# Fourteen projection tiles of a fused decoder block in seven pairs, each by seven block products, with the attention's data through DRAM

## The chip, the cores and the metric

The kernel runs on one core of a Trainium2 chip. A core has a matrix engine (TensorE, PE in the profile; PEld is its weight load), VectorE (DVE), ScalarE (ACT), GpSimd (POOL) and SyncE (SP), which here only issues transfers. Matrix results land in PSUM, a small memory of eight banks; operands lie in SBUF. The metric is the device time in microseconds (us), the median of several runs.

## The reference, cut to what matters

One decoder block over 1024 tokens of width 1024:

```python
h = rms_norm(x, norm_w) * (1 + scale) + shift
proj = h @ w_in
qa, ka, va, za, beta_in, a_in, qb, kb, vb, zb, ga, gb = split(proj)
# mixer A: 8 heads of 128, convolution and SiLU on q, k, v, gated delta rule in chunks
y_A = (headwise_rms_norm(gated_delta_rule(q, k, v, g, beta)) * silu(za)) @ P_A
# mixer B: 12 heads of 64 in three groups with dilations 1, 4 and 16
#   (group 1: token t sees t-128..t; group 2: every 4th; group 3: every 16th)
y_B = (softmax_weighted(dilated_window_attention(qb, kb, vb)) * silu(zb)) @ P_B
merged = sigmoid(ga) * y_A + sigmoid(gb) * y_B
x = rms_norm(x + gate * (merged @ w_out), final_norm_w)
```

All of it is in float32, and the result is compared at that precision.

## The kernel before

**Tiles.** The modulated input h is kept transposed: eight tiles `hT[kk]` of 128 features x 1024 tokens. To keep float32 precision on the faster matmul format, every operand is split into a rounded part `hi` and a remainder `lo` (`activation` Copy on ACT, then a subtraction on DVE), and a product is three matmuls: hi x hi, hi x lo, lo x hi (`three`, line 593). A projection tile is 128 output features x 1024 tokens: 8 feature blocks x 3 terms x 2 halves of 512 tokens, 48 matmuls of 128x512 into the two banks of one `pj` buffer. Its weights arrive in a `wr` buffer (`w_load`, line 572), are split into two `wh` buffers (`w_split`, line 580), and its result goes to a consumer from `finish` (line 727).

**Order of the projections.** `prog` lists them: two gate tiles, then the tiles of the delta rule with gates between them (`ORDER`), then the last 18: query and key tiles of the three attention groups (q, k, q, k for each), then six z tiles. `projections` (line 772) works the list off. `out_store` (line 744) takes a buffer for the result before each tile; for the first query tile of a group it waits until `big` has four to spare.

**Buffers.** SBUF holds 34 `big` buffers of 128 x 1024 floats (16 of them are hT), 6 `mid` of half that, 2 `wr`, 6 `wh`. PSUM holds two `pj` of two banks and four `sb` of one.

**Who decides the order.** The file writes out every engine's instruction order itself. `Sched` (line 110) keeps a clock for each engine from a cost for each operation, and a list of streams (Python generators) with priorities; at each step it lets the ready stream of the smallest number go on. Projections have priority 99: they fill what the recurrences (3), the merges (3.5), the attention (6 to 7) and the splits for the output products (8) leave. On the chip each engine runs its instructions strictly in the order written, waiting where an operand is late. All transfers but one are issued by SP, in one queue.

**Attention.** `attn_group` (line 1319) loads the group's values from DRAM into two buffers, waits for its two query and two key tiles and for the group before, and lets two workers run eight units (`attn_unit`, line 1239): scores of two blocks of 128 queries for two heads, masked minimum on DVE, exponent on ACT, transposes on PE, product with the values, copy into `OG`. When all are done, `combine` (line 1364) weighs the groups against each other; `apply_gate` multiplies by z, `yb_split` splits.

**The tail.** `tail_products` (line 1580): the A branch's output product (`pa`, 8 tiles, reading `YA` from `ya_split`), the B branch's (`pb`, 8 tiles of 36 matmuls, reading `YB`), and the final product with `w_out`.

Of the kernel before, what the change touches and what calls it, by code (L numbers as in the profile page):

```python
# [30 lines left out]
)  # L31
NW = 8
# [17 lines left out]
class Slots:  # L50
# [28 lines left out]
    def put(self, n=1, t=None):  # L79
        for _ in range(n):  # L80
            self.free_at.append(self.s.cur_last() if t is None else t)

# [177 lines left out]
def hybrid_block_kernel(ctx: ExitStack, tc: tile.TileContext, x, c, norm_w, ada_w, ada_b, w_tiles, w_vb0, w_vb1,  # L260
# [50 lines left out]
    Xb = [const([P, 8, 64], f"Xb{i}") for i in range(2)]  # L311
# [7 lines left out]
    gate_d = [dp.tile([P, T], F32, name=f"gd{j}") for j in range(16)]  # L319
    row_d = dp.tile([1, T], F32, name="rowd")  # L320
# [81 lines left out]
    def consts_start():  # L402
        dve.memset(pw[:, 0], -0.5)
        dve.memset(pw[:, 1], 0.5)
        for i in range(2):
            pool.memset(TT[i], 0.0)
            pool.memset(Xb[i], 0.0)
        dve.memset(one_row, 1.0)
        yield ev_row

        pb = yield from pj.get()
        for hf in range(2):
            pe.matmul(pb[:, hf * 512:hf * 512 + 512], one_row, scb[1][0:1, hf * 512:hf * 512 + 512], start=True, stop=True)
        yield
        act.activation(pb, pb, AF.Silu)
        scb[2] = pb
        S.set(ev_mod)
        yield
        scb[0] = yield from big.get()
        act.activation(scb[0], pb, AF.Copy)  # L420
        big.put()
# [149 lines left out]

    def w_load():
        yield ev_loaded
        for u in units[FIRST:]:
            u.raw = yield from wr.get(shape=[P, u.n])
            sp.dma_start(u.raw, u.src)
            S.set(u.raw_ev)
            yield S.now()

    def w_split():  # L580
        for u in units[FIRST:]:
            yield u.raw_ev
# [9 lines left out]

    def three(pt, whi, wlo, khi, klo, first, last):
        for w, m, a, z in ((whi, khi, first, False), (whi, klo, False, False), (wlo, khi, False, last)):
            for hf in range(2):
                sl = slice(hf * 512, hf * 512 + 512)
                pe.matmul(pt[:, sl], w, m[:, sl], start=a, stop=z)
            yield S.now()


# [5 lines left out]
    QB, KB, VB, ZB = {}, {}, {}, {}  # L606
    ev_qb = [Event() for _ in range(6)]
    ev_kb = [Event() for _ in range(6)]
    ev_vb = [Event() for _ in range(3)]
    ev_zb = [Event() for _ in range(6)]  # L610
# [40 lines left out]
    def qk_out(pt, store, i, scale, ev):  # L651
        g = i // 2
        dst = store[i]
        if g:
            r = 4 if g == 1 else 8
            dst = dst.rearrange("p (r u) -> p r u", r=r)
        act.activation(dst, perm(pt, g), AF.Copy, scale=scale)
        pj.put()
        S.set(ev)
        return  # L660
        yield
# [10 lines left out]
    GT = {}  # L672
# [45 lines left out]
    for g_ in range(3):  # L718
        for i_ in (0, 1):
            feat("qB", 2 * g_ + i_)  # L720
            feat("kB", 2 * g_ + i_)
    for i_ in range(6):
        feat("zB", i_)
    for _ in range(len(gates)):
        gate_tile()

    def finish(kind, idx, pt):
# [8 lines left out]
        if kind == "zB":  # L736
            return silu_out(pt, ZB, idx, ev_zb[idx])
        if kind == "qB":
            return qk_out(pt, QB, idx, -0.125, ev_qb[idx])
        if kind == "kB":  # L740
            return qk_out(pt, KB, idx, 1.0, ev_kb[idx])
        return gate_out(pt, idx if kind == "gA" else 8 + idx)

    def out_store(kind, idx):
        st = dict(kA=KT, qA=QT, vA=VT, zA=ZT, qB=QB, kB=KB, zB=ZB, gA=GT, gB=GT)[kind]
        i = idx + 8 if kind == "gB" else idx
        add = dict(kA=4 - idx % 2, qA=1, qB=(4, 0, 4, 0, 4, 0)[idx % 6]).get(kind, 0)
# [24 lines left out]
    def projections():  # L772
# [39 lines left out]
        for n, (kind, idx, u) in enumerate(prog):  # L812
            if n < FIRST:
                continue
            lastp = n == len(prog) - 1
# [26 lines left out]
            if lastp:  # L842
                S.set(ev_tail)
            pt = yield from pj.get()
            yield u.ev
            for kk in range(8):
# [3 lines left out]
                if lastp:  # L850
                    big.put(2)
            wh.put(2)
            S.add(finish(kind, idx, pt), 10, f"{kind}{idx}")

        yield from tail_products()
# [57 lines left out]
    ev_ttfree = [Event() for _ in range(H)]  # L913
    kss = const([P, H, 8], "kss")
# [320 lines left out]
    OG = {}  # L1235
# [3 lines left out]
    def attn_unit(g, i2, ti):  # L1239

        qt, kt = QB[2 * g + ti], KB[2 * g + ti]
        tiles = []
        for i in (2 * i2, 2 * i2 + 1):
            prev = (g == 0 and i > 0) or (g == 1 and i % 2 == 1)
            tiles.append((i, i % 2, (i - 1) * P if prev else i * P, 256 if prev else 128))
        pbs = []
        for hd in range(2):
            pb = yield from sb.get()
            pbs.append(pb)
        for i, a, k0, nk in tiles:  # L1250
            for hd in range(2):
                r = slice(64 * hd, 64 * hd + 64)
                pe.matmul(pbs[hd][:, a * 256:a * 256 + nk], qt[r, i * P:(i + 1) * P], kt[r, k0:k0 + nk], start=True,
                          stop=True)
        yield
        sms = []
        for hd in range(2):
            h4 = 2 * ti + hd
            sm = yield from mid.get()
            sms.append(sm)  # L1260
            for i, a, k0, nk in tiles:
                msk = amask2 if g == 2 else amask if nk == 256 else amask[:, P:2 * P]
                dve.tensor_tensor_reduce(sm[:, a * 256:a * 256 + nk], pbs[hd][:, a * 256:a * 256 + nk], msk, 1.0, 3e38,
# [9 lines left out]
        for hd in range(2):  # L1273
# [7 lines left out]
            mid.put()  # L1281
            pt = yield from mid.get()
# [6 lines left out]
        for i, a, k0, nk in tiles:  # L1289
            nb = nk // P  # L1290
            for b in range(nb):
                ki = k0 // P + b
                for hd in range(2):
                    h4 = 2 * ti + hd
                    vv = VB[g][ki // 4].rearrange("p (a f) -> p a f", a=4)[:, ki % 4, h4 * 64:h4 * 64 + 64]
# [4 lines left out]
        dve.tensor_copy(OG[g][ti][:, 2 * i2 * P:2 * (i2 + 1) * P], pb[:, 0:2 * P])  # L1300
        sb.put()
        mid.put(2)
# [4 lines left out]
    def v_load(g, q, t):  # L1307

        t4 = t.rearrange("p (a f) -> p a f", a=4)
        if g == 0:  # L1310
            sp.dma_start(t4, vb_d[g].rearrange("(i p) f -> p i f", p=P)[:, 4 * q:4 * q + 4])
        elif g == 1:
            src = vb_d[g].rearrange("(b p r) f -> r p b f", b=2, r=4)
            for a in range(2):
                sp.dma_start(t4[:, 2 * a:2 * a + 2], src[2 * q + a])
        else:
            sp.dma_start(t4, vb_d[g].rearrange("(p r) f -> p r f", r=8)[:, 4 * q:4 * q + 4])

    def attn_group(g):
        yield [ev_vbd[g], ev_qb[2 * g]]  # L1320
        VB[g] = []
        for q in range(2):
            t = yield from big.get(owed=1)
            v_load(g, q, t)
            VB[g].append(t)
        S.set(ev_vb[g])
        yield [ev_vb[g], ev_qb[2 * g], ev_qb[2 * g + 1], ev_kb[2 * g], ev_kb[2 * g + 1]]
        if g:
            yield ev_og[g - 1]
        OG[g] = []  # L1330
        for q in range(2):
            t = yield from big.get(owed=1)
            OG[g].append(t)
        todo = [(i, ti) for i in range(4) for ti in range(2)]
        live = [0]

        def worker():
            while todo:
                i, ti = todo.pop(0)
                yield from attn_unit(g, i, ti)  # L1340
            live[0] -= 1

        for q in range(2):
            live[0] += 1
            S.add(worker(), 6, f"attn{g}w{q}")
        yield ev_og[g]
        yield lambda: live[0] == 0
        big.put(6)
# [15 lines left out]
    def combine(g):  # L1364
        yield ev_sg
        yield ev_yas[7]
# [43 lines left out]
        rows4 = fg_d[g].rearrange("(h i) p -> h (i p)", h=4)  # L1410
        for ti in range(2):
            og = OG[g][ti]
            for q in range(2):
                sl = slice(q * 512, q * 512 + 512)
                fx = yield from mid.get()
                for hd in range(2):
                    sp.dma_start(fx[64 * hd:64 * hd + 64, :],
                                 rows4[2 * ti + hd:2 * ti + hd + 1, sl].to_broadcast([64, 512]))
                yield
                dve.tensor_tensor(og[:, sl], fx, og[:, sl], op=OP.mult)  # L1420
                mid.put()
            S.add(apply_gate(g, ti), 7.6, f"apply{g}{ti}")

    def apply_gate(g, ti):
        yield ev_zb[2 * g + ti]
        z, og = ZB[2 * g + ti], OG[g][ti]
        if g == 0:
            dve.tensor_tensor(z, og, z, op=OP.mult)
        else:
            r = 4 if g == 1 else 8  # L1430
            dve.tensor_tensor(perm(z, g), perm(z, g), og.rearrange("p (r u) -> p r u", r=r), op=OP.mult)
        big.put()
        S.set(ev_yb[2 * g + ti])
# [23 lines left out]
    def ya_split():  # L1457
        yield ev_tail
        while ya_todo:
            h = ya_todo.pop(0)  # L1460
            yield ev_ya[h]
            ts = []
            for q in range(2):
                t = yield from mid.get()
                sp.dma_start(t, ya_d[h][:, q * 512:q * 512 + 512])
                ts.append(t)
            yield
            hi = yield from big.get(F32R)
            lo = yield from big.get(F32R)
            for q in range(2):  # L1470
# [8 lines left out]

    def yb_split():  # L1480
        yield ev_m[0]
        for i in range(6):
            yield ev_yb[i]
            yield from split(YB, i, ZB[i], ev_ybs[i], add=0)
# [214 lines left out]
    for g in range(3):  # L1699
        S.add(combine(g), 7.5, f"combine{g}")  # L1700
    S.add(ya_split(), 8, "yas")
    S.add(ya_split(), 8.1, "yas")
    S.add(yb_split(), 8, "ybs")
    S.add(wo_split(), 8, "wos")
    S.add(rows_stream(), 9, "rows")
    S.add(projections(), 99, "proj")
# [3 lines left out]
def _layout(inp):  # L1710
# [20 lines left out]
    am = np.where((dist >= 0) & (dist <= P), 0.0, BIG)  # L1731
    am2 = np.where((r >= cc) & (r % 2 == cc % 2), 0.0, BIG)
# [40 lines left out]
```

## Time and profile before

| what | value |
|---|---|
| median of 3 runs | 1286.85 us (1286.12 to 1287.16) |
| the profiled execution | 1286.06 us |
| its span, first to last instruction | 1284.3 us |
| PE busy | 1264.3 us, 98% |
| DVE, ACT, POOL busy | 688.9, 485.6, 148.5 us |
| granted PE clock, mean | 0.998 of full speed |
| moved by DMA | 137.65 MB, 107 GB/s on average |
| chain of waits that ended last | PE 83%, issue 7%, DVE 5% |

Helpers record every operation, so nearly all rows carry the line L103; instructions are told apart by the buffers they write and read (`pj<-big,wh` is a projection or output product, `sb` rows on PE are recurrence and attention). A group row ends with busy time, the mean duration of one instruction in ns, and the idle time ahead of it with its releaser. A matmul's duration contains the pipeline, so the distance from start to start says what one costs in a row. In the timeline, neighbouring instructions of one form are merged into a row with their count.

### The profile page before, as it was taken

To read this page: it belongs to the slowest core of one execution; us is meant where nothing else is said; L and a number is where in the kernel's file an instruction comes from. 1 tells how busy PE (TensorE), PEld (TensorE's weight loads), DVE (VectorE), ACT (ScalarE), POOL (GpSimd) and SP (SyncE) were. 2 spreads that over 40 slices of the span, in tenths; PEclk is the share of its full clock that TensorE was granted. 3 is DMA by queue.
4 is the path that set the end of the run, shared out by engine and by line. 5 is a ranking of instruction groups with operands and counts; after the bars stand their busy time and mean duration, and the time that the engine had idled before them with its cause. 6 is when DMAs were issued, how large, how long until landed. Compare 5 with 4: busy or idle time off the path is not lost.

```text
span 1284.3 us, 18871 instructions
## 1 busy us (share of the span) xinstructions
PE 1264.3 (98%) x7386; PEld 1044.5 (81%) x7386; DVE 688.9 (54%) x1426; ACT 485.6 (38%) x1042; POOL 148.5 (12%) x113
## 2 busy tenths in 40 slices
PE   7999999999999999999999999999999999999997
PEld 3689888998888988888888888877787888888886
DVE  5955793257873367863678634232322157645533
ACT  5524622346233354234452343353536441222211
POOL 4700300023000212000220002000000000002400
PEclk9999999999999999999999999999999999999999
DMA  9534432153321262331423314302011257243422
GB/s 358 193 129 132 121 96 78 34 169 99 112 78 38 82 197 53 95 100 67 140 74 105 93 48 150 99 18 80 21 51 34 67 184 209 95 144 118 149 95 85
DMA packets 76138, 137.65 MB, mean 107 GB/s; under 512 B 30193, under 2 KB 43921, under 8 KB 76050
## 3 DMA queue, kind: packets, MB, share of 16 engines
q1 hardware_dynamic: 75906, 136.20, 33.4%
q8 instruction: 58, 0.95, 0.3%
q14 instruction: 30, 0.25, 0.1%
q10 hardware_dynamic: 144, 0.26, 0.1%
HBM read 105.84 MB, written 30.59 MB: 106 GB/s over the span
## 4 chain that ended last, share of the span: by engine, by line
PE 83%; issue 7%; DVE 5%; DMA 2%; ACT 1%; POOL 1%; SPq 0%; POOLq 0%; DVEq 0%; ACTq 0%
PE pj L103 69%; PE sb L103 14%; DVE big L103 3%; DMA big<-grow 1%; ACT big L103 1%; DVE mid L103 1%; DVE wh L103 1%; POOL big L103 1%; ACT wh L103 0%; DMA big<-otd 0%; DMA big<-vtd 0%; POOL mo L103 0%; DMA otd<-big 0%; DMA vtd<-big 0%; SPq L103 0%
## 5 line engine op out<-in xcount | busy, mean ns | idle before, releaser
L103 PE MATMUL pj<-big,wh 128*128 128x512 f32 x3776 | 922.7, 397 | 0.0
L103 PEld LDWEIGHTS pj<-big,wh 128*128 128x128 f32 x3776 | 692.9, 188 | 145.8 <-issue 11.0
L103 ACT ACTIVATE wh<-wr 128x1024 fp32r<-128x1024 f32 (+2 forms) x92 | 93.2, 1013 | 314.1 <-PE pj L103 300.7
L103 DVE TENSOR_TENSOR wh<-wr,wh 128x1024 fp32r<-128x1024 f32 (+2 forms) x89 | 114.2, 1284 | 145.0 <-ACT wh L103 144.8
L103 ACT ACTIVATE big<-big 128x1024 f32<-128x1024 f32 (+1 forms) x61 | 64.6, 1058 | 149.2 <-DVE big L103 119.4
L103 PE MATMUL pj<-wh,big 128*128 128x256 f32 (+2 forms) x702 | 109.8, 307 | 0.2 <-DVE big L103 0.2
L103 PEld LDWEIGHTS pj<-wh,big 128*128 128x128 f32 x702 | 96.1, 189 | 5.5 <-issue 0.4
L103 DVE SCALAR_TENSOR_TENSOR big<-pj,cw,big 128x1023 f32<-128x1023 f32 (+2 forms) x72 | 92.0, 1278 | 1.7
L103 PE MATMUL sb<-sq,big 128*128 128x128 f32 x464 | 66.2, 276 | 0.5 <-DVE sq L103 0.2
L103 PEld LDWEIGHTS sb<-sq,big 128*128 128x128 f32 x464 | 62.1, 191 | 5.5 <-ACT sq L103 0.9
L103 DVE TENSOR_TENSOR big<-big,big 128x1024 f32<-128x1024 f32 (+3 forms) x40 | 54.9, 1381 | 14.9 <-ACT big L103 12.8
L103 ACT ACTIVATE mid<-sb 128x384 f32<-128x384 f32 (+5 forms) x75 | 34.1, 461 | 67.2 <-PE sb L103 66.8
L103 ACT ACTIVATE big<-pj 128x1024 f32<-128x1024 f32 (+1 forms) x53 | 48.6, 917 | 18.4 <-PE pj L103 18.3
L103 POOL TENSOR_TENSOR wh<-wr,wh 128x1024 fp32r<-128x1024 f32 x3 | 8.2, 2723 | 388.9 <-ACT wh L103 388.9
L103 DVE COPY big<-sb 128x256 f32<-128x256 f32 (+1 forms) x32 | 12.4, 388 | 74.2 <-PE sb L103 74.1
L103 ACT ACTIVATE mid<-mid,sta 128x128 f32<-128x128 f32 (+1 forms) x96 | 42.2, 441 | 25.5 <-DVE sta L103 25.4
L103 PE MATMUL pj<-big,big 128*128 128x512 f32 x210 | 49.1, 389 | 0.0
L103 ACT ACT_TABLE_LOAD x29 | 37.2, 1283 | 30.6 <-DVE big L103 25.8
L103 DVE SCALAR_TENSOR_TENSOR sq<-sq,gsm,sb 128x128 f32<-128x128 f32 x48 | 16.5, 345 | 59.2 <-PE sb L103 57.7
L103 PEld LDWEIGHTS pj<-big,big 128*128 128x128 f32 x210 | 39.4, 188 | 8.2
L103 DVE TENSOR_TENSOR mid<-big 64x31 f32<-64x31 f32 (+15 forms) x124 | 41.2, 332 | 8.9 <-POOL big L103 5.5
L103 POOL TENSOR_TENSOR mo<-mo,pw 128x8 f32<-128x8 f32 x8 | 13.1, 1636 | 283.4 <-DVE mo L103 283.3
(131 smaller groups left out, 1135.4 us busy)
## 6 DMA issues: line engine op xcount, KB each, us to landing
wr<-in_w_tiles_dram SPq DMA_DIRECT2D x64, 512.0 KB, 3.9
big<-in_ada_w_dram SPq DMA_DIRECT2D x24, 512.0 KB, 9.0
big<-in_x_dram SPq DMA_DIRECT2D x16, 512.0 KB, 4.7
gd<-big SPq DMA_DIRECT2D x16, 512.0 KB, 5.0
big<-gd SPq DMA_DIRECT2D x16, 512.0 KB, 4.8
big<-grow SPq DMA_DIRECT2D x8, 512.0 KB, 5.5
vtd<-big SPq DMA_DIRECT2D x8, 512.0 KB, 2.7
big<-vtd SPq DMA_DIRECT2D x32, 128.0 KB, 4.1
```

Of the source, the lines that this page charges most:

```text
L103: r = f(*a, **k)
```

## The change

**Seven products for eight.** Two projection tiles are one matrix of 256 output features x 1024 input features, and h is one of 1024 x 1024. Cut into 2 x 2 blocks (A of 128 x 512, B of 512 x 512), the product normally takes eight block products. The change takes seven, on sums of blocks (the Strassen-Winograd scheme): S and T are sums of weight and of h blocks. Of the last 18 tiles four z tiles now go first, as single tiles; then seven pairs: queries and keys of group 1, 2 and 3 (`a0 b0 a2 b2 a4 b4`), and the last two z tiles (`z8`).

**Weights.** `w_combine` forms S1 to S4 of a pair on DVE (two of them in place in the `wr` buffers, two in the merges' old buffer `Xb2`) and splits them: seven `wh` buffers a pair instead of four.

**Blocks of h.** `h_sums` forms T1 to T4 on DVE and POOL, from hi + lo, after the last triangular inverse (`BLK`), four `mid` at a time, and stores them in DRAM. `h_blocks` loads T2, T3, T4 into twelve `big` buffers as these come free and splits them; T1 goes over the second halves of `hT[0..3]` once the last single tile has read them.

**Products.** `pair` runs the seven in the order A11 B11, A12 B21, S2 T2, S3 T3, S1 T1, S4 B22, A22 T4, 12 matmuls each. B11, T2 and T1 add up in one `sb` bank that is held through all pairs; B21 has one half of a `pj` buffer, T3 and T4 add up in the other; B22 takes one more `sb` bank. `pair_out` copies the bank by ACT after B11, T2 and T1 into `mid`, adds on DVE, and sends four quarter results to DRAM, for groups 2 and 3 reordered by the dilation.

**Attention.** Queries, keys, values and results pass through DRAM. A unit takes two `big` buffers, loads its own pieces with three transfers, and stores its result. Three workers take the 24 units in order; a unit waits for its own query and key tile and for the T4 blocks. The factor -0.125 moves from the query evacuation into the masking operation, and the masks change sign with it. `combine` no longer waits for the A branch; `yb_split`, now two streams, loads attention result and z, weighs, gates and splits. `ya_split` takes its two `big` buffers ahead of its `mid` buffers and loads, and waits for spare ones, four more while the attention runs.

The diff, cut to its core:

```diff
+SINGLE = "z2 z3 z4 z5"
+PAIRS = "a0 b0 a2 b2 a4 b4 z8"
+PRODUCTS = (("A11", "B11"), ("A12", "B21"), ("S2", "T2"), ("S3", "T3"), ("S1", "T1"), ("S4", "B22"), ("A22", "T4"))
+BLK = "x3"
+BLK1 = "T1 T3 T3 T5"
+WORKERS = 3
+RESERVE = 4
+HPRIO = 8
...
+    def w_combine(u):
...
+        yield from begin(u.raws[0], "A11", "A12")
+        yield u.raw_ev[1]
+        a21, a22 = u.raws[1][:, 0:half], u.raws[1][:, half:]
+        S.add(sums(), 2, "sums")
+        yield ev_s2
+        yield from begin(ss[:, 0:u.n], "S2", "S1")
+        yield ev_s3
+        yield from begin(u.raws[1], "S3", "A22")
+        yield ev_s4
+        yield from begin(a11, "S4")
...
+    def pair(u, blocks, ready, sink, free=None):
...
+        for a, b in PRODUCTS:
+            if b in ("B11", "T2", "T1"):
+                pt = bank
+            elif b == "B21":
+                t = yield from pj.get()
+                pt = t[:, HALVES[0]]
+            elif b in ("T3", "T4"):
+                pt = t[:, HALVES[1]]
+            else:
+                pt = yield from sb.get()
+            ps[b] = pt
+            wait = before if b == "B11" else read[dict(T2="B11", T1="T2", T4="T3")[b]] if b in ("T2", "T1", "T4") else None
+            if wait:
+                yield wait
...
+            for kt in range(nk):
+                yield ready[b][kt]
...
+                pe.matmul(pt, whi, hi, start=kt == 0 and b not in ("T2", "T1", "T4"), stop=False, **how)
+                pe.matmul(pt, whi, lo, start=False, stop=False, **how)
+                pe.matmul(pt, wlo, hi, start=False, stop=kt == nk - 1, **how)
...
+        p = yield from copy("B11")
+        yield done["B21"]
+        yield from add("B21", p, 0, 0, True)
+        u = yield from copy("T2")
+        v = yield from copy("T1")
+        yield from add("T3", v, 1, 1, False)
+        S.set(read["T3"])
+        yield done["B22"]
+        yield from add("B22", v, 0, 1, True)
+        sb.put()
+        yield done["T4"]
+        yield from add("T4", u, 1, 0, True)
+        pj.put()
...
     def out_store(kind, idx):
-        st = dict(kA=KT, qA=QT, vA=VT, zA=ZT, qB=QB, kB=KB, zB=ZB, gA=GT, gB=GT)[kind]
+        if kind in ("zB", "qB", "kB"):
+            BT[kind, idx] = yield from big.get(add=0)
+            return
...
     def attn_unit(g, i2, ti):
-        qt, kt = QB[2 * g + ti], KB[2 * g + ti]
+        i0 = 2 * i2
+        kf = max(i0 - 1, 0) if g == 0 else i0
+        n_ = i0 + 2 - kf
+        buf, sm2 = yield from big.many(2)
...
+        sp.dma_start(qt, qb_d[2 * g + ti][:, i0 * P:(i0 + 2) * P])
+        sp.dma_start(kt, kb_d[2 * g + ti][:, kf * P:(i0 + 2) * P])
...
+        sp.dma_start(v3, src[:, :, ti * P:(ti + 1) * P])
...
+        sp.dma_start(og_d[2 * g + ti][:, 2 * i2 * P:2 * (i2 + 1) * P], pts[0][:, 0:2 * P])
...
     def combine(g):
         yield ev_sg
-        yield ev_yas[7]
...
+            yield lambda: len(big.free_at) > big.debt + 1 + (0 if ev_og[2].t else RESERVE)
             hi = yield from big.get(F32R)
             lo = yield from big.get(F32R)
+            ts = yield from mid.many(2)
```

453 lines of the change are left out of this document (326 added, 127 removed).

## The prediction

> **What bounds the kernel now.** I read the page's totals first, then busy time by stage, then the matrix engine in order of time.
>
> ```profile
> span 1284.3 us, 18871 instructions
> PE 1264.3 (98%) x7386; PEld 1044.5 (81%) x7386; DVE 688.9 (54%) x1426; ACT 485.6 (38%) x1042; POOL 148.5 (12%) x113
> PE 83%; issue 7%; DVE 5%; DMA 2%; ACT 1%; POOL 1%; SPq 0%; POOLq 0%; DVEq 0%; ACTq 0%
> ```
> ```profile
> core 0: us, PE busy (x) PEld busy (x) DVE busy (x) ACT busy (x) POOL busy (x), PEclk, DMA share, GB/s
> 642.00:780.50 138.50, 137.13 (x896) 114.83 (x895) 90.19 (x200) 55.74 (x139) 12.01 (x8) 1.00 0.27 79
> 780.50:824.70 44.20, 44.20 (x197) 36.34 (x195) 12.32 (x17) 8.91 (x11) 5.89 (x4) 1.00 0.39 131
> 824.70:1037.00 212.30, 212.30 (x1275) 163.88 (x1275) 57.90 (x235) 104.51 (x281) 0.00 (x0) 1.00 0.20 60
> 1037.00:1124.00 87.00, 87.00 (x386) 71.77 (x385) 55.04 (x85) 23.13 (x32) 0.00 (x0) 1.00 0.49 151
> ```
>
> The last 18 projection tiles fill 780.5 to 1037: PE is busy in all of it, DVE 27% and ACT 49% of the second stretch. So PE work taken out here shortens the kernel by its own length, until something else makes PE wait. A busy PE is not yet one at its peak, so the price of a matmul comes from starts:
>
> ```profile
> start us, us, engine line op out<-in xcount [idle before <-releaser]
> 1197.99 8.32 PE L103 MATMUL pj<-big,big 128*128 128x512 f32 x36
> 1206.15 1.52 PE L103 MATMUL pj<-wh,big 128*128 128x512 f32 x6
> ...
> 1267.35 3.56 PE L103 MATMUL sb<-big,big 128*128 128x512 f32 x15
> 1270.75 1.56 PE L103 MATMUL sb<-wh,big 128*128 128x512 f32 x9
> ```
>
> The first two starts lie 8.16 us apart for 36 matmuls, 0.2267 us each, in tiles that alternate between two banks. The last two lie 3.40 us apart for 15 that all accumulate in one bank: 0.2267 again. A block product does the second, so I charge it no more.
>
> **Term 1: fewer matmuls.** A pair of tiles takes 2 x 48 = 96 matmuls of 512 columns. Seven products of 4 blocks x 3 terms take 84. Seven pairs drop 84, and 84 x 0.2267 = **-19.0 us**. The Trainium skill, "TensorE: Matmul & The Clock Gate", Part 1, gives 215.7 ns for a warm back-to-back matmul of this size; the saving by that figure would be 18.1 us. The trace differs (226.7 ns), and it decides.
>
> **Term 2: an unfilled stretch.** Ahead of the 18 tiles the last two recurrences run without projection matmuls:
>
> ```profile
> 759.56 0.38 PE L103 MATMUL sb<-sq,TT 128*128 128x128 f32 x2
> 759.70 0.71 PE L103 MATMUL pj<-big,wh 128*128 128x512 f32 x2
> ...
> 764.57 0.39 PE L103 MATMUL sb<-sq,TT 128*128 128x128 f32 x2
> ...
> 772.35 0.87 PE L103 MATMUL sb<-sq,TT 128*128 128x128 f32 x4
> 773.30 2.32 PE L103 MATMUL sb<-sq,big 128*128 128x128 f32 x16
> 775.68 0.88 PE L103 MATMUL sb<-sq,TT 128*128 128x128 f32 x4
> ...
> 778.25 1.16 PE L103 MATMUL pj<-big,wh 128*128 128x512 f32 x4
> ```
>
> A chunk of both heads takes 5.01 us with 12 projection matmuls in it (759.56 to 764.57, rows of 2, 2, 4 and 4), which leaves 5.01 - 2.72 = 2.3 us of its own. Bare, it takes 3.33 us (772.35 to 775.68). So three bare chunks hide about 3 us of waiting that the profile calls busy. The code says why: `out_store` asks `big` for four spare buffers before the first query tile. The single z tiles that now come first ask for none. They may find a buffer from 769 on, or the block loads may take it: 0 to -3, I take **-1.5**.
>
> **Term 3: work beside PE.**
>
> ```profile
> L103 DVE TENSOR_TENSOR wh<-wr,wh 128x1024 fp32r<-128x1024 f32 x72 | 98.7, 1371 | 122.7 <-ACT wh L103 122.6
> L103 DVE TENSOR_TENSOR big<-mid,big 128x512 f32<-128x512 f32 x12 | 8.1, 690 | 4.6 <-DMA mid<-fgd 4.6
> L103 ACT ACTIVATE wh<-wr 128x1024 fp32r<-128x1024 f32 x75 | 79.3, 1058 | 232.7 <-PE pj L103 219.4 <-DMA mid<-fgd 9.9 <-DMA wr<-in_w_tiles_dram 1.9
> L103 ACT ACTIVATE mid<-sb 128x512 f32<-128x512 f32 x12 | 7.1, 596 | 10.6 <-PE sb L103 10.6
> L103 ACT ACT_TABLE_LOAD x29 | 37.2, 1283 | 30.6 <-DVE big L103 25.8 <-DVE mid L103 2.6 <-DMA big<-grow 1.0
> ```
>
> A pair needs on DVE three wide splits, half a split, four weight sums and four additions out of PSUM: 3 x 1.37 + 9 x 0.69 = 10.3 us, against 2 x 1.37 = 2.7 for two tiles. That adds 7 x 7.6 = 53 us. On ACT it needs 3 x 1.06 + 4 x 0.60 = 5.6 us, about 1.5 more than now. Splitting the sums of h adds 8 x 0.69 of DVE and 16 x 0.60 of ACT. DVE rises to (57.9 + 53 + 6) / 196 = 60% of the stretch, ACT to some (104.5 + 11 + 10) / 196 = 64%. Neither becomes the bound. The sums themselves (24 half-width DVE operations, 17 us) fall before 780, where DVE is at 90.2 of 138.5; what they delay there is the recurrences, behind which 4 x 10.9 us of single tiles stand as filler. I cost them nothing; uncovered, up to 17.
>
> **Term 4: hand-overs inside a pair.** A product is 12 x 0.2267 = 2.72 us. Three products add onto a bank that must first be read. The tightest is the last one: T1's result is copied by ACT (0.60) and added by DVE (0.69) while one product runs. With hops of some 0.3 that is 1.6 of 2.7 us. It fails only when ACT stands in a table load (1.28) or DVE in a wide split (1.37): 1.1 us of slack is then short by 0.2, or by 1.6 if both meet. Bounds 0 and 7 x 1.6 = 11; with the two engines near 60%, I take 0.4 a pair, **+3**. Behind a waiting matmul the whole PE queue stands, attention included.
>
> **Term 5: DRAM trips.**
>
> ```profile
> wr<-in_w_tiles_dram SPq DMA_DIRECT2D x64, 512.0 KB, 3.9
> mid<-yad SPq DMA_DIRECT2D x16, 256.0 KB, 5.4
> big<-gd SPq DMA_DIRECT2D x16, 512.0 KB, 4.8
> nd<-big SPq DMA_DIRECT2D x32, 32.0 KB, 1.7
> ```
>
> Each attention unit now issues three loads and a store on SP, where weights and gates queue too; none is shown before, so I use 4 to 5.5 us to landing. DMA runs at 20% of the stretch and takes some 32 MB more (24 tiles of 512 KB and 16 half tiles, each written and read). Stores of the third group write pieces of 256 bytes; the nearest rows, 1.7 us for 32 KB in pieces of 128 bytes and 5.4 for 256 KB, leave 2 to 14 us (eight times the first), within the 19 us of a pair. The Trainium skill, "DMA: Bandwidth & Descriptors", Specifications, speaks against that form: below 512 bytes the engines read, modify and write. By it these eight stores would be near my upper end; no run so far shows this form.
>
> Does attention still end in time?
>
> ```profile
> 824.71 1.58 PE L103 MATMUL sb<-big,big 64*128 64x128 f32 x16
> ...
> 875.60 17.98 PE L103 MATMUL pj<-big,wh 128*128 128x512 f32 x78
> ```
> ```profile
> 1045.08 3.60 SPq L103 DMA_DIRECT2D mid<-std x6
> ```
> ```profile
> 1072.55 0.69 DVE L103 TENSOR_TENSOR big<-mid,big 128x512 f32<-128x512 f32 x1
> ```
>
> Eight units took 50.9 us with two workers, 6.4 us a unit. Attention's own PE time in the stage is 212.3 - 672 x 0.2267 = 60 us. In the new order pair b0 ends near 779 + 4 x 10.9 + 2 x 19.0 = 861, b4 near 977 (two more pairs and 20 us of attention each time), the projections near 1006 (one pair and 10 us of attention), the first output product 87 us and the other 10 us later, at 1103. At 6.4 us a unit three workers finish by 977 + 5 + 51 = 1033; storing takes some 8 and combining 27.5 (1045.08 to 1072.55), so gating starts near 1068; six tiles in three rounds of two, some 7 us each by the loads and DVE rows above, end near 1090. The slack is some 13 us.
>
> The other late reader is the A branch: `ya_split` now waits for buffers that the last pair frees only in its third product, and then loads. The eight tiles need about 20 us and are consumed over 16 x 1.36 = 22. Uncovered by attention, I work out 11 us of waiting; covered, none. I take **+1**.
>
> **Sum.** -19.0 - 1.5 + 3 + 1 = -16.5. The profiled execution took 1286.06 us (span 1284.3 and 1.76 around it), so 1269.6; the median of the runs is 0.8 higher: **1270**.
>
> **Rivals.** *The hand-overs eat it:* if most pairs lose near the upper 11 us of term 4 and the A branch its 11, the time is 1286.9 - 20.5 + 22, about 1288; with half of that, 1278. For it: long operations on both engines, six `mid` buffers shared by copies, sums and A loads. Against: 1.1 us of slack everywhere. *Attention starves the second product, slower than before:* a pair holds two of the four `sb` banks, one of them throughout. If a unit takes u us from 861 on, the last gated tile is ready at 861 + 24u + 57 (8, 27.5 and 22 from above) and is wanted 6.8 us into the second product, at 1110. It is late from u = 8.0, and the gain is gone at 8.7. Scaling 6.4 by 4/3 for the lost bank gives 8.5; at 9.5 the kernel ends at 1270 + 24 x 1.5 = 1306. Against: a third worker, and two workers spend their time in latencies rather than waiting for banks. *It does not do what it says:* the copies force extra PE waits at each pair's start because split weights find no `wh` slot (seven needed, six there): one split, 2.7 us, seven times, gives 1289. Against: the seventh is wanted only when the first two are free.
>
> **Chances.** Forecast with its own range 1264 to 1276: 0.60. Partly eaten by hand-overs (1276 to 1284): 0.20. No difference: 0.08, from the upper ends of the same rival and the weight slots. Attention late and slower: 0.12. A measurement of this kernel can tell 0.2%, 2.6 us, from no change. So faster 0.80, same 0.08, slower 0.12. Leaving out the last two cases, the range is 1264 to 1284.
>
> **What would show it.** Right: 84 fewer matmuls of 128x512 at the same 0.2267; PE without idle from 820 to 1100; query and key loads landing within 6 us; projection matmuls in 769 to 778. Wrong: PE waiting for ACT or DVE on `sb` or `pj` by over 0.5 us a pair; `pb` matmuls waiting for a `big` tile near 1100; POOL or DVE ending the wait ahead of the first `T` product; DVE above 70% of the stretch.

## The result, and the profile after

The changed kernel takes 1278.82 us (median of 10 runs, 1276.79 to 1284.46), the one before 1287.41 beside it: ratio 0.9935, 95% interval 0.992 to 0.995. It is 8.6 us faster; I had forecast about 17 (1270 against 1286.85). The direction was right; the forecast gain was twice what came. The page of the profiled execution (1279.4 us):

```profile
span 1277.7 us, 19213 instructions
PE 1252.2 (98%) x7302; PEld 1030.8 (81%) x7302; DVE 766.9 (60%) x1528; ACT 497.9 (39%) x1079; POOL 173.9 (14%) x128
PE 88%; DVE 3%; DMA 3%; ACT 2%; issue 2%; POOL 1%; SPq 0%; POOLq 0%; ACTq 0%; DVEq 0%
```

PE still bounds the kernel and has 84 instructions fewer. Groups of the kernel before, then of the one after (busy us, mean ns, idle ahead):

```profile
L103 PE MATMUL pj<-big,wh 128*128 128x512 f32 x3776 | 922.7, 397 | 0.0
```
```profile
L129 PE MATMUL pj<-big,wh 128*128 128x512 f32 x3356 | 825.2, 398 | 0.8 <-DVE big L129 0.5 <-DVE ik L129 0.2
L129 PE MATMUL sb<-big,wh 128*128 128x512 f32 x368 | 105.1, 423 | 0.0
```

The 14 tiles took 48 matmuls each, and a pair now takes 36 in `pj`: 3776 less 14 x 48 plus 7 x 36 is 3356. The pairs' other 7 x 48 = 336 are in the second row, beside 32 of the first gate tiles. Busy time by stretch, after and before:

```profile
core 0: us, PE busy (x) PEld busy (x) DVE busy (x) ACT busy (x) POOL busy (x), PEclk, DMA share, GB/s
642.00:780.50 138.50, 138.50 (x900) 116.81 (x899) 93.77 (x200) 56.24 (x126) 11.11 (x7) 1.00 0.34 96
867.60:1014.00 146.40, 145.92 (x912) 109.50 (x911) 81.06 (x230) 86.33 (x228) 0.00 (x0) 1.00 0.54 156
1014.00:1046.00 32.00, 28.64 (x179) 20.93 (x180) 14.97 (x58) 21.31 (x73) 0.00 (x0) 0.95 0.68 232
1115.00:1185.00 70.00, 69.45 (x306) 56.87 (x305) 40.68 (x33) 18.70 (x19) 11.17 (x5) 1.00 0.41 136
```
```profile
1014.00:1046.00 32.00, 32.00 (x143) 26.51 (x142) 11.41 (x15) 14.01 (x19) 0.00 (x0) 1.00 0.56 188
```

The second recurrence stretch (642 to 780) is now full. The last attention units (1014 to 1046) are not: PE stands 3.4 us, and its mean granted clock is 0.95 of full speed.

Since a busy PE is not one at its peak, I also added up, over all neighbouring matmul starts of a trace, by how much each distance exceeds the usual one for its shape (0.2267 for 128x512; for each shape the median of the kernel before). I call this sum the excess. It is worked out from the starts, not a view of the profile, and not all of it is loss: the attention's stretch has 24.0 in the kernel before, where PE never stands. Us by stretch:

| kernel | to 430 | 430–642 | 642–824.5 | 824.5–1046 | from 1046 | all |
|---|---|---|---|---|---|---|
| before | 31.4 | 3.7 | 7.3 | 24.0 | 0.1 | 66.4 |
| after | 31.4 | 9.9 | 3.0 | 32.4 | 2.0 | 78.7 |
| after less before | 0.1 | 6.2 | -4.3 | 8.4 | 1.9 | 12.3 |

-19.0 + 12.3 = -6.7, the difference of the two profiled executions (1286.06 and 1279.4). So 12 of the 19 us were lost again, in the main at two places, and the experiments ask why; the 1.9 from 1046 on I did not follow. (One profile is one execution: where the order of the instructions is the same, the first stretch varies between 30.6 and 35.4 from run to run, and 824.5–1046 between 28.6 and 33.4 among later runs with one order, queues aside. So times are compared by their medians.)

**The loss near 450.** I must first correct what I wrote of the kernel: "after the last triangular inverse (`BLK`)" holds for the loading of the blocks alone. The sums themselves follow `BLK1`, the merges 1, 3, 3 and 5, each of which closes just as a pair of recurrences begins. GpSimd's part of them in the trace after:

```profile
199.30 1.28 POOL L129 TENSOR_TENSOR mid<-big,big 128x512 f32<-128x512 f32 x1
...
406.05 2.97 POOL L129 TENSOR_TENSOR mid<-big,big 128x512 f32<-128x512 f32 x2 [18.32 <-DVE mid L129]
```

From 238 us on, behind the first portion, the written-out order on PE differs from the one before. Projection matmuls fill where a recurrence is held up, and are missing later: counted from the starts, PE had begun 1610 of them (`pj` with `wh`) by 430 us, and 212 matmuls of the recurrences (those with `sq`), against 1562 and 264 before. So the recurrence lasts to 458 us instead of 440, and at its end, shortly after the second and third portion, this happens on PE:

```profile
448.64 0.71 PE L129 MATMUL sb<-sq,big 128*128 128x128 f32 x4 [0.23 <-DVE sq L129]
...
451.39 0.49 PE L129 MATMUL sb<-sq,big 128*128 128x128 f32 x2 [1.80 <-ACT sq L129]
...
452.47 1.22 PE L129 MATMUL sb<-sq,big 128*128 128x128 f32 x4 [0.37 <-ACT sq L129]
453.34 1.20 PE L129 MATMUL pj<-big,wh 128*128 128x512 f32 x2
454.34 1.05 PE L129 MATMUL sb<-sq,big 128*128 128x128 f32 x4
```

The recurrence runs bare, 2.4 us idle in three pieces; then two matmuls of 512 columns take 1.00 from start to the next (454.34 less 453.34) where 0.45 is usual. Before, there is dense work here, first as a row, then the stretch by windows, before and after; the last two rows show the place in the change more finely:

```profile
439.77 11.04 PE L103 MATMUL pj<-wh,big 128*128 128x256 f32 x90
```
```profile
448.00:457.00 9.00, 9.00 (x52) 7.91 (x51) 6.60 (x12) 4.19 (x5) 0.00 (x0) 1.00 0.86 272
```
```profile
448.00:457.00 9.00, 6.61 (x33) 5.47 (x32) 3.97 (x12) 3.96 (x13) 2.21 (x2) 0.81 0.87 282
448.60:452.01 3.41, 1.57 (x10) 1.28 (x10) 1.61 (x4) 2.51 (x7) 0.00 (x0) 1.00 0.74 217
452.01:455.42 3.41, 3.04 (x12) 2.64 (x12) 1.41 (x6) 1.08 (x5) 0.71 (x1) 0.50 1.06 338
```

The granted clock was a half for 3.41 us, right behind 3.41 us in which PE was busy for 1.57. The Trainium skill, "TensorE: Matmul & The Clock Gate", Part 1, has the clock go to half after an idle window of about 3.4 us. Here less idle time than that was enough: the longest single wait was 1.80 us.

**The loss near 1030.** What PE waited for most from 1010 to 1050 (us in total, times, longest), the rows around its longest wait, the load in the chain of waits that ended last (start, us, what), and the windows on both sides of the wait's end:

```profile
PE sb L129 <- DMA big<-kbd: 2.2, 3, 1.8
```
```profile
1028.73 1.13 PE L129 MATMUL sb<-big 64*128 64x128 f32 x8 [1.76 <-DMA big<-kbd]
1029.79 4.17 PE L129 MATMUL pj<-big,wh 128*128 128x512 f32 x12
1033.89 0.71 PE L129 MATMUL sb<-big 64*128 64x128 f32 x8
```
```profile
1021.69 6.90 DMA big<-kbd
```
```profile
1025.46:1028.87 3.41, 1.39 (x13) 0.86 (x13) 1.14 (x3) 0.78 (x3) 0.00 (x0) 1.00 0.91 317
1028.87:1032.28 3.41, 3.41 (x14) 2.70 (x15) 2.14 (x10) 2.56 (x9) 0.00 (x0) 0.50 0.90 273
```

A unit's key load took 6.90 us to land (the median of such key loads is 3.1; the prediction's sign of being right was 6 at most), and the 12 matmuls behind the wait need 4.10 us for 12 x 0.2267 = 2.72: half clock again, as at 450.

### The profile page after: what moved, and what is told of

It reads as the page before. It is cut to its first block, busy times and chain, and to the rows that moved or that the text cites. A ratio compares the mean times of both kernels' runs of the same rounds, so it can differ in the third digit from the quotient of the medians.

```text
span 1277.7 us, 19213 instructions
## 1 busy us (share of the span) xinstructions
PE 1252.2 (98%) x7302; PEld 1030.8 (81%) x7302; DVE 766.9 (60%) x1528; ACT 497.9 (39%) x1079; POOL 173.9 (14%) x128
## 4 chain that ended last, share of the span: by engine, by line
PE 88%; DVE 3%; DMA 3%; ACT 2%; issue 2%; POOL 1%; SPq 0%; POOLq 0%; ACTq 0%; DVEq 0%
PE pj L129 67%; PE sb L129 22%; DVE big L129 2%; ACT big L129 1%; DMA wr<-in_w_out_dram 1%; DMA big<-kbd 1%; POOL big L129 1%; DMA big<-gd 0%; ACT wh L129 0%; DVE mid L129 0%; DVE wh L129 0%; DMA wr<-in_w_pa_dram 0%; POOL wh L129 0%; ACT L129 0%; SPq L129 0%
## 5 line engine op out<-in xcount | busy, mean ns | idle before, releaser
L129 PE MATMUL pj<-big,wh 128*128 128x512 f32 x3356 | 825.2, 398 | 0.8 <-DVE big L129 0.5
L129 PEld LDWEIGHTS pj<-big,wh 128*128 128x128 f32 x3356 | 617.2, 189 | 131.9 <-issue 9.9
L129 ACT ACTIVATE wh<-wr 128x1024 fp32r<-128x1024 f32 (+3 forms) x99 | 97.5, 985 | 239.7 <-PE pj L129 223.1
L129 DVE TENSOR_TENSOR wh<-wr,wh 128x1024 fp32r<-128x1024 f32 (+3 forms) x96 | 115.2, 1200 | 64.2 <-ACT wh L129 64.0
L129 ACT ACTIVATE big<-big 128x1024 f32<-128x1024 f32 (+2 forms) x77 | 74.1, 969 | 187.2 <-DVE big L129 133.3
L129 PE MATMUL sb<-big,wh 128*128 128x512 f32 x368 | 105.1, 423 | 0.0
L129 PEld LDWEIGHTS sb<-big,wh 128*128 128x128 f32 x368 | 66.9, 190 | 21.1 <-issue 8.4
L129 DVE TENSOR_TENSOR big<-big,big 128x1024 f32<-128x1024 f32 (+4 forms) x44 | 57.8, 1316 | 25.9 <-ACT big L129 18.8
L129 ACT ACTIVATE big<-sb 128x512 f32<-128x512 f32 (+2 forms) x80 | 40.9, 522 | 39.6 <-PE sb L129 39.5
L129 PE MATMUL sb<-cst,big 128*128 128x128 f32 x268 | 43.5, 284 | 8.0 <-DVE rstd L129 4.9
```

The lines of the kernel that those rows point to most:

```text
L129: r = f(*a, **k)
```

## The experiments

Ratios are to the kernel before on the same chip, with their 95% intervals.

### The first set: which part loses

**The change again.**

> The changed kernel once more, beside the others of this set: 1278.8 us as before, 8.6 under the kernel before. It is the mark that the next three are read against.

1279.06 us, 0.9936 [0.9921, 0.9951]; 10.1 us of excess in 430–642 and 31.8 in 824.5–1046. Both losses recur.

**The sums of h late,** after the last merge:

```diff
-BLK1 = "T1 T3 T3 T5"
+BLK1 = "T7 T7 T7 T7"
```

> The sums T1 to T4 of h are all formed after the last merge of the delta rule instead of after merges 1, 3, 3 and 5, where they stand among the recurrences. Theory: what the prediction put at nothing, the sums beside the recurrences, costs some 6 us (PE idles near 450 and again after 470 in the changed kernel, not in the kernel before), so 1273 us. Rival: those waits are chance or belong to something else, and the missing gain lies in the pairs or in the tail alone: 1278.8.

1284.68, 0.9981 [0.9967, 0.9996]. The excess of 430–642 falls to 3.7, the value before: the place of the sums made that loss. But the first pair now lacks its blocks:

```profile
837.54 0.79 PE L129 MATMUL pj<-big,wh 128*128 128x512 f32 x1 [8.35 <-ACT big L129]
```

**No seven products.** The 14 tiles go as full tiles of 48 matmuls, with no sums and no blocks of h (twelve `big` buffers are held empty for them until the last tile); the data still pass through DRAM. The core of the edit:

```diff
-        two(o)
+        for i in (0, 1):
+            if o[0] == "z":
+                feat("zB", int(o[1:]) - 8 + i)
+            else:
+                feat("qB" if o[0] == "a" else "kB", int(o[1:]) + i)
```

> The fourteen tiles go as fourteen full products of 48 matmuls again; queries, keys, values, z and results still pass through DRAM, the same twelve buffers are held from the same time on but stay empty, and no sums of h are formed. Theory: seven products save their whole 19.0 us and their hand-overs cost under 1, and the sums cost 6, so this is 13 above the changed kernel, near 1292. Rival: hand-overs inside the pairs eat about half of the saving, and the sums nothing: 9 above it, near 1288, or less.

1290.89, 1.0027 [1.0016, 1.0038]: 11.8 slower than the change. Of 19.0 for the matmuls, 7 were thus paid for the products' own work, the sums of h included. Against the kernel before it loses 3.7 us, and its excess is the old one up to 824.5 apart from the gain behind 642, but 28.1 in 824.5–1046 against 24.0: some 4 us are lost there whether or not there are pairs. The attention through DRAM may be their cause; this run also keeps the new order of tiles, the three workers and the twelve buffers, and nothing tells these apart.

**The attention's result stores on GpSimd's queue.**

```diff
-        sp.dma_start(og_d[2 * g + ti]...
+        other.dma_start(og_d[2 * g + ti]...    # other: GpSimd's queue
```

> The changed kernel with the same written order, but the 24 stores of attention results are issued by GpSimd's queue instead of SP's, so that SP no longer stands at a store while the loads behind it wait. Theory: SP's order is what starves the A branch and the last attention units between 1011 and 1046, where PE loses 8 to 10 us: about 1274. Rival: the last attention group and the A tiles are late of themselves (too little other work is left for PE there), and the queue changes little: 1278.8, within 1.5.

1277.63, 0.9927 [0.9912, 0.9942]; excess of 824.5–1046 28.5 for 32.4, but 11.2 in 430–642. By the medians it is 1.4 us faster, within the intervals: the place of the stores on SyncE's queue is a small part at most.

### The second set: where the sums go, and the order of the attention

**The sums behind the last inverse** (what I had believed the code to do), and **behind the recurrences** instead of ahead of them:

```diff
-BLK1 = "T1 T3 T3 T5"
+BLK1 = "x3 x3 x3 x3"      # the first
+BLK1 = "t1 t3 t3 t5"      # the second
```

> All sums of h are formed once the last triangular inverse is stored (about 717 us), beside the last merges and the last recurrence pair only. With the sums after merge 7, PE lost nothing near 450 any more but 12 us near 835, where the first T blocks came late. Theory: both losses are the same 17 us of VectorE work looking for a place; some 25 us earlier they are in time for the first pair, so the loss near 450 (4.6, and 1.6 after 470) is saved and the one near 835 falls to under 3: 1273 to 1276. Rival: beside the last two recurrences they cost as much as beside the earlier ones: 1279.

> Each of the four portions of sums is formed right after a recurrence has ended (1, 3, 3, 5) instead of right after a merge, when a recurrence is about to begin. Theory: a recurrence is a chain of short VectorE, ScalarE and PE steps, and only there does extra VectorE work reach PE; after it there is slack, so the loss near 450 goes and none appears near 835: 1273. Rival: the portions then stand in front of the next inverses, which are as tight a chain: 1278.8.

The first took 1282.06, 0.9963 [0.9948, 0.9979]: nothing is lost at 450, but the pair starts late, one row for all of it:

```profile
831.98 5.44 PE L129 MATMUL sb<-big,wh 128*128 128x512 f32 x12 [7.93 <-ACT mid L129]
```

The second, called the late sums from here on, took **1274.04, 0.9905 [0.9887, 0.9923]**, 4 to 5 us less than the change (by the ratios 3.9, by the medians 4.8; the two intervals just touch). At 450 there is dense work again, as before:

```profile
445.67 8.16 PE L129 MATMUL pj<-wh,big 128*128 128x256 f32 x66
```

Its excess is 2.9 in 430–642, and 29.0 in 824.5–1046, though the PE instructions of that stretch stand in the same order as in the change. There the unit with the late keys waited 0.40 us for them, and what followed ran at full clock (12 matmuls in 2.95 us):

```profile
1024.43 0.71 PE L129 MATMUL sb<-big 64*128 64x128 f32 x8 [0.40 <-DMA big<-kbd]
1025.07 3.02 PE L129 MATMUL pj<-big,wh 128*128 128x512 f32 x12
1028.02 0.71 PE L129 MATMUL sb<-big 64*128 64x128 f32 x8
```

So a wait longer by 1.4 us cost twice: itself, and the half clock behind it. That this execution was spared is no merit of the late sums: four runs of their order, three with loads or stores on another queue, show 28.6 to 33.4 in this stretch. What belongs to them is the 7 us less in 430–642, with 1.5 more in 642–824.5.

**The groups in reverse order,** and **the A tiles ahead of the attention:**

```diff
-PAIRS = "a0 b0 a2 b2 a4 b4 z8"
+PAIRS = "a4 b4 a2 b2 a0 b0 z8"      # the first, with the units in the same order
-RESERVE = 4
+RESERVE = 2                         # the second,
-    S.add(ya_split(), 8, "yas")
+    S.add(ya_split(), 5.5, "yas")   # with A's two streams at 5.5 and 5.6
```

> The pairs and the attention units go in the order group 3, 2, 1. The units of group 1 have more PE work each (blocks of 256 keys) than those of group 3. Theory: at the end PE lacks work because the last group's units wait for their own loads and chains; with 8 to 10 us more PE work inside them, the 10 us lost between 1014 and 1046 fall by about half: 1274. Rival: a longer last group only ends later and the A tiles still come late: 1278.8 or slower.

> The splits of the A branch's tiles go ahead of the attention units in the written order, and leave two buffers to them instead of four. Theory: PE starves after 1011 because the first output product waits for A tiles; with these first, PE has that product to fill the gaps of the attention: 3 to 6 us less, 1273 to 1276. Rival: the attention then ends later, and the B branch's tiles come late for the second product: no gain, 1278.8 or more.

1290.18, 1.0029 [1.0016, 1.0041], and 1284.46, 0.9982 [0.9970, 0.9994]. Both hopes fell. In the first the excess of 824.5–1046 rises to 34.0, and 10.3 are lost from 1046 on, where the change loses 2.0; in the second it falls to 28.5, and 10.1 are lost from 1046 on.

### The third set: is it the queue or the units in flight?

All on top of the late sums (1274.04). Stores on GpSimd's queue; only the 16 loads of `yad` there; both; four workers:

```diff
-        sp.dma_start(og_d[2 * g + ti]...      +  other.dma_start(...)     # first, third
-                sp.dma_start(ts[q], ya_d[h]...  +  other.dma_start(...)   # second, third
-WORKERS = 3
+WORKERS = 4                                                               # fourth
```

> The sums of h behind the recurrences, and the attention's result stores issued by GpSimd's queue. Base: the version with the late sums alone, 1274.0, ratio 0.9905 of its kernel before. Theory (SyncE's queue is a minor part of the loss between 1014 and 1046): the two gains add, 1.4 less, about 1272.6, ratio 0.9895. Rival (the stores decide nothing once the order of the sums is mended): 1274 again.

> The sums of h behind the recurrences; of the A branch, the 16 loads of `yad` go to GpSimd's queue, the stores stay on SyncE's. Theory A (A tiles come late because their loads stand on SyncE's queue behind the attention's stores and loads): with the loads free the A tiles after 1010 come closer together than 4 to 5 us, 3 to 5 us of the 6 us lost between 1014 and 1046 come back, about 1270. Theory B (the attention's last units have nothing dense beside them because they start 43 us later than before; A tiles wait for buffers, not for the queue): 1274 within 1.5.

> Late sums, and both the attention's result stores and the 16 loads of `yad` on GpSimd's queue. Theory A: about 1269. Theory B: like the stores alone, about 1272.6. If the loads now stand behind stores on the new queue, as they did on the old one: 1274.

> Late sums and four attention workers in place of three, no queue changed. Theory B (the end of the attention is what stands bare after 1014): with one unit more in flight the attention ends some 5 to 10 us earlier and 3 to 5 us come back, about 1270. Theory A (the A loads' place on SyncE's queue): no gain, 1274, or worse, since one more unit takes three `big` buffers from the A tiles.

| run | us | ratio |
|---|---|---|
| stores | 1273.23 | 0.9886 [0.9865, 0.9907] |
| loads | 1276.97 | 0.9914 [0.9890, 0.9937] |
| both | 1272.32 | 0.9896 [0.9867, 0.9924] |
| four workers | 1276.81 | 0.9918 [0.9901, 0.9935] |

No interval lies apart from that of the late sums alone (0.9887 to 0.9923). From the third to the last, the A tiles still come 4.2 to 4.8 us apart on average, as with the late sums alone (4.3). Neither the queue nor the number of units in flight is shown to matter. (A unit takes two `big` buffers, not the three that the last expectation names.)

### The fourth set: is it that the attention comes late?

Before, the attention starts at 824.7; now at 867.6. Here, on top of the late sums, the first group's queries and keys are the four single tiles, and three z pairs come last; then the same with a z pair between; then the first with no buffers held back from the A tiles:

```diff
-SINGLE = "z2 z3 z4 z5"
-PAIRS = "a0 b0 a2 b2 a4 b4 z8"
+SINGLE = "q0 q1 k0 k1"
+PAIRS = "a2 b2 a4 b4 z10 z12 z8"    # first, third
+PAIRS = "a2 b2 z10 a4 b4 z12 z8"    # second
-RESERVE = 4
+RESERVE = 0                         # third
```

> On top of the sums behind the recurrences: the four single tiles are the first group's queries and keys, and three pairs of z tiles come last, so that the attention can start near 825 and its last units have 57 us of dense matmuls beside them. Theory B (the late attention is the cause): the 6 us lost at 1014 to 1046 come back, about 1268. Theory C (the A tiles come late after the last pair, whatever the attention does): the attention ends early, but PE then waits for A tiles alone, without attention matmuls to fill in: 5 to 12 us of PE idle at the first output product, 1276 to 1282.

> As the one before, but one of the z pairs stands between the second and the third group's pairs, so that the attention starts early and still has its last units at the end. Theory B: half of the 6 us back, about 1271. Theory C: 1274 within 2, since the last units fill the wait for the A tiles as they do now.

> The attention early and three z pairs last, as in the first of this set, with no `big` buffers held back from the A tiles (RESERVE 0). If buffers held for the attention set the A tiles' pace: 3 to 6 us faster than that one. If the last pair's own buffers do (theory C): within 2 us of it. Theory B says nothing here beyond 1268.

1295.14, 1.0057 [1.0042, 1.0072]; 1290.59, 1.0022 [1.0010, 1.0034]; 1288.01, 1.0007 [0.9996, 1.0018]. The time that theory B forecast did not come. PE at the first unit and after the attention's matmuls are over, then ACT, in the first of them:

```profile
825.17 1.65 PE L129 MATMUL sb<-big 64*128 64x128 f32 x8 [3.90 <-DMA big<-kbd]
...
1051.95 10.32 PE L129 MATMUL pj<-big,wh 128*128 128x512 f32 x33 [3.25 <-ACT big L129]
```
```profile
1034.17 1.29 ACT L129 ACTIVATE big<-mid 128x512 fp32r<-128x512 f32 x2 [5.29 <-DMA mid<-yad]
```

The last A tile is complete at 1053.3, with the late sums alone at 1035.2, and now nothing fills the wait. That was worse than theory C allowed (1276 to 1282). The attention's excess was not saved but stands elsewhere: 7.8 us in 824.5–867.6, where the change shows 0.4 and the kernel before 7.2. And a new wait came in, 3.90 us for the first unit's keys (its 780–824.5 has 4 us more), so this is no clean test of the attention's place. The third run, with the buffers given to the A tiles, is 7 us faster than the first: its middle A tiles come up to 9 us sooner, its last no sooner (1053.7). The buffers held for the attention pace them in part.

### The fifth set: the buffers, or the A tiles' own path?

On top of the late sums: no reserve; the same with stores and `yad` loads on GpSimd's queue; and A tiles that aren't split (both halves are loaded whole from `yad`, so the A part of the output is not the reference's; `mid`, ACT and DVE are out of their path, the matmuls are the same).

```diff
-RESERVE = 4
+RESERVE = 0                                        # first, second
-            ts = yield from mid.many(2)
...
+            sp.dma_start(hi.bitcast(F32), ya_d[h])  # third
+            sp.dma_start(lo.bitcast(F32), ya_d[h])
```

> The sums behind the recurrences, and no `big` buffers held back from the A tiles (RESERVE 0 in place of 4). If the shared `big` buffers pace the A tiles: they come earlier, but the attention then waits for buffers, and its last units end later; 1274 less 2 to 4 if the A tiles are the shorter side, about 1271. If their own path paces them: 1274 within 1.

> As the one before, with the attention's result stores and the `yad` loads on GpSimd's queue: about 1270, the sum of the pieces that have not cost anything so far (1272.3 with the queues and RESERVE 4, less 2). If buffers decide nothing: 1272.

> The sums behind the recurrences; the A tiles are not split: both halves are loaded straight from `yad` into their `big` buffers (the small half then holds a copy of the whole, so the A part of the output is not the reference's), which takes `mid`, two ACT copies and two DVE subtractions a tile out of their path and adds one load of 512 KB. The matmuls are the same. If that path paces them: the tail's 6 us fall to about 2, about 1270. If the `big` buffers do: 1274 within 2.

1275.08, 0.9900 [0.9880, 0.9921]; 1277.43, 0.9925 [0.9902, 0.9949]; 1276.76, 0.9917 [0.9901, 0.9933]. None is faster than the late sums alone. The third gives no sign that the splitting paces the tiles, though a gain could hide behind the added load of 512 KB. The first did move the wait. Its last A tile, its windows in the old place, and PE at the second output product:

```profile
1023.51 1.29 DVE L129 TENSOR_TENSOR big<-mid,big 128x512 fp32r<-128x512 f32 x2 [0.52 <-issue]
```
```profile
1014.00:1046.00 32.00, 31.94 (x195) 23.41 (x194) 14.92 (x55) 16.75 (x58) 0.00 (x0) 1.00 0.52 171
1109.00:1120.00 11.00, 6.58 (x19) 4.75 (x18) 7.33 (x6) 2.96 (x3) 0.00 (x0) 0.69 0.23 75
```
```profile
1111.45 0.77 PE L129 MATMUL pj<-big,wh 128*128 128x512 f32 x2 [2.18 <-ACT big L129]
1114.46 5.74 PE L129 MATMUL pj<-big,wh 128*128 128x512 f32 x15 [2.25 <-DVE big L129]
```

The A tiles are complete at 1024.8 and PE no longer waits in 1014–1046; then the B branch's tiles are late, with 4.4 us of waiting and a half clock behind it. The excess is 26.5 in 824.5–1046 (29.0 with the reserve) and 8.6 from there on (1.5): by this run, what the A branch gets from the pool of `big` is paid by the B branch's tiles.

## Why the prediction was right and wrong

Forecast: -19.0 - 1.5 + 3 + 1 = -16.5. Between the two profiles: -19.0 for the matmuls, -4.3 for the unfilled stretch, +6.2 beside the recurrences, +8.4 in the attention's stretch, +1.9 behind it and 0.1 ahead, together -6.7.

- **Term 1, 84 matmuls at 0.2267: right.** The counts fell by 84. Without the seven products the kernel is 11.8 us slower, not 19.0, because the products' other work (next points) goes with them.
- **Term 2, the unfilled stretch: right in mechanism, too small.** -1.5 was forecast, bounds 0 and -3; 642–824.5 gained 4.3 and 642 to 780 shows no PE idle. The sum had counted the 3 us hidden in busy time and left out the 1.4 idle in its own row (137.13 of 138.50); together they come to the gain. The changed kernel without pairs and sums has it too (2.9 for 7.3), as it must if the single z tiles bring it.
- **Term 3, "I cost them nothing": this step failed first.** The sums of h were said to fall where DVE has room, with the recurrences as all that they delay, covered by single tiles. I had read their place wrongly, and priced their engine time instead of what they do to the order: the projection matmuls were used up ahead of the recurrence's end, and 430–642 lost 6.2. Moving the portions behind the recurrences gave 4 to 5 us back (1274.04, against 1270 forecast); putting them where I had thought them to be cost a wait of 7.93 us at the first pair. The engine shares had been right: from 867.6 to 1014, DVE is busy 81.06 of 146.4, 55% (60 forecast), ACT 59% (64).
- **Term 4, hand-overs, +3: too high where it can be seen.** The first two pairs run without attention:

```profile
824.42 2.88 PE L129 MATMUL sb<-big,wh 128*128 128x512 f32 x12
...
865.46 2.20 PE L129 MATMUL pj<-big,wh 128*128 128x512 f32 x9
867.59 0.93 PE L129 MATMUL sb<-big 64*128 64x128 f32 x8
```

  189 matmuls from 824.42 to 867.59 are 43.17 us, 0.3 above 189 x 0.2267. The hand-over rival, with "1.1 us of slack everywhere" against it, fell. In the other five pairs hand-overs can't be told from the attention; PE stands 0.5 us in all from 867.6 to 1014.
- **Term 5, "covered, none. I take +1": mis-sized.** The stretch lost 8.4, against 4 forecast for terms 4 and 5 together. About 4 are there without pairs too. Another 3.4 are what the change lost there and the late sums' profile did not, in the same order: a load that landed late and the half clock behind it, which differs from run to run. What was mis-sized is the A branch: eight tiles were to need about 20 us, 2.5 each. Splits of the third and the eighth A tile in the change:

```profile
1015.25 1.29 DVE L129 TENSOR_TENSOR big<-mid,big 128x512 fp32r<-128x512 f32 x2
...
1039.81 1.29 DVE L129 TENSOR_TENSOR big<-mid,big 128x512 fp32r<-128x512 f32 x2
```

  Five tiles in 24.6 us are 4.9 each, where the prediction had PE take one in 2 x 1.36 = 2.7; so PE lacks dense work beside the attention's last units. That the A branch waits for buffers was named; that relief there can be paid at the B tiles was not.
- **The rivals.** The time came where half of the hand-over rival had put it (1278), but not by hand-overs; that is chance. Attention starving the second product did not come: 1115 to 1185 shows 0.55 us of idle. The second product did wait for its tiles once the A tiles got their buffers without reserve, so the place was right and the cause (PSUM banks) was not shown. Weight slots costing 2.7 us a pair fell with the two pairs above, which leave no room for it.
- **The stores in pieces of 256 bytes,** 2 to 14 us: the third group's keys against the first's, 3.1 to 2.2 us to landing, from windows 930 to 990 and 840 to 870.

```profile
kbd<-mid SPq DMA_DIRECT2D x4, 256.0 KB, 2.2
...
kbd<-mid SPq DMA_DIRECT2D x4, 256.0 KB, 3.1
```

  The reading, modifying and writing that the Trainium skill, "DMA: Bandwidth & Descriptors", Specifications, names for pieces below 512 bytes shows here as no more than the 0.9 us between them; the upper end was far off.

**What stays open.** The late sums alone leave 5 us more excess in 824.5–1046 than before. Without the pairs some 4 are there too, so most of it seems to belong to what these runs share. It follows neither queue, workers nor the splitting, as far as the intervals tell, and fewer buffers held back only move it. A larger pool was not tried, nor a third stream of `ya_split`: the two that there are load a tile only when they are done with their last, which could set the pace of 4 to 5 us as well. The best versions, late sums (1274.04) and those with the stores on GpSimd's queue as well (1273.23; with the A loads, 1272.32), beat both kernels and can't be told from each other.

## What to carry to other kernels

Price side work not only by engine time but by what it does to a written-out order: moving four portions of sums by one stage was worth 4 to 5 of 19 us. Where buffers are shared out to the last one, relief for one reader can show up as another's wait, so follow it past the stage in which it was gained. Where PE stands for more than half of a few microseconds, look for half clock behind it and price it too.

## What the hardware showed that I had not expected

Waits of 1.76 and 1.80 us, with little PE work around them, were followed by half the clock (12 matmuls in 4.10 us for 2.72), so that such a wait cost about double. Both times it was half for 3.41 us, right behind 3.41 us in which PE was busy for 1.39 and 1.57. The same unit's keys, 0.40 us late in another run, brought none.
